# Four held weight-row pairs of the second feed-forward matrix: one transfer per two column halves instead of one per pair

## The chip, the cores and the metric

The kernel runs on one core of one Trainium2 chip. The metric is the device time of one execution, in microseconds (us). Before the change the median of three executions is 1231.31 us (1231.11 to 1232.1). The profile that is read below is one profiled execution, which took 1231.44 us. Engines go by short names: PE is the matrix engine and PEld its weight load, DVE the vector engine, ACT the scalar engine, POOL the GpSimd engine, SP the sync engine, whose queue issues most of the transfers.

## The reference

Two decoder layers over 256 tokens of width 1024. Each layer is a half-step feed-forward block, a mixer (gated attention and gated spatial mixing) and a second half-step feed-forward block, each followed by a layer norm:

```python
for l in range(DEPTH):                                   # DEPTH = 2
    h = _swiglu(x, ffn_w1[l, 0], ffn_w3[l, 0], ffn_w2[l, 0])
    x = _layernorm(ALPHA * x + 0.5 * h, ln_g[l, 0], ln_b[l, 0])
    h = _mixer(x, l, ...)
    x = _layernorm(ALPHA * x + h, ln_g[l, 1], ln_b[l, 1])
    h = _swiglu(x, ffn_w1[l, 1], ffn_w3[l, 1], ffn_w2[l, 1])
    x = _layernorm(ALPHA * x + 0.5 * h, ln_g[l, 2], ln_b[l, 2])

def _swiglu(x, w1, w3, w2):                              # w1, w3: 1024 x 2816, w2: 2816 x 1024
    return (jax.nn.silu(x @ w1) * (x @ w3)) @ w2
```

All is float32. The change touches `... @ w2`, which runs four times in the program, once in each feed-forward block.

## The kernel before

**Number format.** A float32 matrix product is made of three products of a shorter format. Each operand is split into a high part (a copy, on ACT) and a low part (operand minus high part, on DVE); PE then adds high x high, high x low and low x high (`three`, L214). A weight transfer is 1 MB, 128 x 2048 floats, into one of 4 `raw` buffers; `stream` splits it in two blocks of 1024 columns, each by one ACT copy (`whi`, L172) and one DVE subtraction (`wlo`, L174). High and low blocks live in two pools of 8 buffers each. A transfer can be issued when its `raw` buffer is free, that is after the last DVE subtraction that reads it.

**Order.** On PE the instructions run in the order in which the program writes them. On the other engines a planner puts each engine's instructions in an order ahead of time, by its own estimate of when operands are ready and, among those ready, by a priority that rises with each transfer (`step`), so that what the program writes earlier goes first. `issue_after` edges (`behind`, `after`) fix some places: in the stage after a norm, the second block of the second weight transfer and all of the third come behind the first token tile's normalisation (`norm.ends[0]`), those of the fourth behind the low part of the second transposed half (`norm.xlo[0, 1]`).

**The second feed-forward matrix.** Its 2816 rows are 22 tiles of 128 rows. Five pairs of row tiles (`SQ`) go through a seven-product scheme (`stream_s`, tiles `shi`, `slo`, `shh`, `shl`), whose sums stand in seven PSUM banks S1 to S7. The other six pairs (`PQ`) are plain. Output is two token tiles t by two column halves c of 512; the four results collect in `ends[t, c]`. The first two plain pairs are multiplied between the seven-product pairs. The other four are *held*: they are transferred and split, but multiplied only at the end, result by result: (0,0) with all four pairs, then (0,1), (1,0), (1,1). A pair and a column half take 6 matmuls, a result 24. Before the change a transfer holds one pair: its first column half in the first block, its second in the second block.

**Folds.** After the last seven-product pair, the banks S1, S5, S6 and S7 are folded into the residual on DVE: `ln.more` (L479, L477), `u` (L667) and `v` (L668), with one ACT copy (L664). In the program they stand ahead of the held transfers, but for the last three, which stand behind them.

**The norm and the next stage.** When a result is complete, `ln.part` adds it to the residual (L486) and takes its statistics (L491). After both halves of a token tile, `finish` aggregates (L498), takes an inverse square root in a chain of 128 x 1 operations (L186 to L192) and normalises the two halves (L502). PE then transposes the normalised halves (L546), ACT scales and copies them (L552, L179), DVE takes their low parts (L180), and the next stage's matmuls read them. The four transposes of a half stand at fixed places of the PE order: those of tile 0 after 6 and after 24 matmuls of the result (1,1), those of tile 1 in the next stage (after 30 and 42 of its matmuls). The next stage's first four weight transfers are split in blocks of 512 columns (`llo`, `lhi` for the first six, `wlo`, `whi` for the other ten). The last feed-forward block has no next stage; it writes the output.

Of the kernel before, what the change touches and what calls it, by code (L numbers as in the profile page):

```python
# [17 lines left out]
ALU = mybir.AluOpType  # L18
# [13 lines left out]
NS = 5  # L32
SQ = [(FB + 2 * p, FB + 2 * p + 1) for p in range(NS)]
PQ = [(k, k + 1) for k in (0, 2, *range(FB + 2 * NS, FT, 2))]
HEADS = 8
HD = 64
GROUPS = 8
# [19 lines left out]
def trunk(ctx, tc, x, xT, w13a, w13b, w2s, w2p, wb, wqk, wa, wbr, wo, gateb, sgug, sgub, sguwT, sgubias, lam, diffg,  # L57
# [18 lines left out]
    def name(s):  # L76
        serial[0] += 1
        return f"{s}_{serial[0]}"
# [32 lines left out]
    def step():  # L111
        chunk[0] += 1
        tc.cur_priority = chunk[0] * STEP
# [35 lines left out]
    def behind(ins):  # L149

        return tc.issue_after(ins) if ins is not None else nullcontext()

    def stream(src, width=CH, sub=HC, lent=(), after=(None, None)):

        step()
        raw = raw_pool.tile([P, CH], F32, tag="raw", name=name("raw"))
        nc.sync.dma_start(raw[:, :width], src)
        out = []  # L160
        for o in range(0, width, HC):
            if o // HC in lent:
                hi, lo = ([act.tile([P, 512], F32R, tag="slot", name=name(n)) for _ in range(2)] for n in ("lhi", "llo"))
                at = [(hi[j], lo[j]) for j in range(2)]
            else:
                hi = hi_pool.tile([P, HC], F32R, tag="hi", name=name("whi"))
                lo = lo_pool.tile([P, HC], F32R, tag="lo", name=name("wlo"))
                at = [(hi[:, p : p + sub], lo[:, p : p + sub]) for p in range(0, HC, sub)]
            for p, (h, w) in zip(range(0, HC, sub), at):
                r = raw[:, o + p : o + p + sub]  # L170
                with behind(latest[0]):
                    A.activation(h, r, AF.Copy)  # L172
                with behind(after[o // HC] or latest[1]):
                    V.tensor_tensor(out=w, in0=r, in1=h.bitcast(F32), op=ALU.subtract)  # L174
            out.append((hi, lo))
        return out
# [78 lines left out]
    def rows_p(ps, t, q, piece, xh, xl, c0=0, n=512, stop=False, start=False):  # L255

        for j, k in enumerate(q):
            wh, wl = (v[:, j * 512 + c0 : j * 512 + c0 + n] for v in piece)
            three(ps[:, :n], xh(k)[:, t * P : (t + 1) * P], xl(k)[:, t * P : (t + 1) * P], wh, wl,
                  start and j == 0, stop and j == 1)  # L260
        beat(n / 1024)
# [133 lines left out]
    b = side_bank()  # L395
# [169 lines left out]
    def ffn(l, f, i, norm, last=False):  # L565
        xh, xl = parts(both)
        h_hi, h_lo = ({q: act.tile([P, 512], F32R, tag="slot", name=name(n)) for q in PQ} for n in ("hhi", "hlo"))
        p_hi, p_lo = h_hi, h_lo
        h_hi, h_lo = ({k: d[q][:, j * T : (j + 1) * T] for q in PQ for j, k in enumerate(q)} for d in (h_hi, h_lo))
        hh, hl = h_hi.get, h_lo.get  # L570
# [59 lines left out]
        for j in range(FR, FT, 2):  # L630
            qa = s512("qa")
            for m, z in gemm_a2([w13a[l, f, j - FR + m] for m in range(2)], both, lambda m: t512("silu"), bank=side_bank):
# [5 lines left out]
        ln = Norm(l, i, 2.0 * ALPHA, 4.0 * EPS, qa[:, :1], last)  # L638
        S = {n: side_bank() for n in (3, 7, 4)}
        S.update({n: bank() for n in (1, 2, 5, 6)})  # L640
        ends = {(0, 0): [(S[2], 0, 512)], (0, 1): [(S[3], 0, 512)], (1, 0): [(S[4], 0, 512)],
                (1, 1): [(side_bank(), 0, 512)]}
        pair, held, plain = None, [], list(PQ)

        def plain_pair(hold):
            q = plain.pop(0)
            w = stream(w2p[l, f, PQ.index(q)])
            if hold:
                held.append((q, w))
                return  # L650
            for c in range(2):
                for t in range(NT):
                    for ps, o, m in ends[t, c]:
                        rows_p(ps, t, q, w[c], hh, hl, o, m, start=q == PQ[0] and t + c == 2)

        for n, q in enumerate(SQ):
            pair, w = stream_s(w2s[l, f, n], pair)
            for b in (1, 2, 5, 6, 3, 7, 4):
                three(S[b], *s_op[q][b], *w[b], n == 0, n == NS - 1 and b in (1, 5, 6, 7))
            beat(1.75)  # L660
            if n < 2:
                plain_pair(False)
        u, v = s512("u"), s512("v")
        A.activation(u, S[6], AF.Copy)  # L664
        ln.more(1, 0, S[7], ALU.subtract, ln.scale)
        ln.more(0, 0, S[1], ALU.add, ln.scale)
        V.tensor_tensor(out=u, in0=u, in1=S[1], op=ALU.add)  # L667
        V.tensor_tensor(out=v, in0=S[5], in1=u, op=ALU.subtract)  # L668
        ln.more(0, 1, v, ALU.add, ln.scale)
        while plain:  # L670
            plain_pair(True)
        ln.more(1, 1, v, ALU.add, ln.scale)
        ln.more(1, 0, u, ALU.add)
        ln.more(1, 1, S[7], ALU.add)
        for t in range(NT):
            for c in range(2):
                for ps, o, n in ends[t, c]:
                    for q, w in held:
                        rows_p(ps, t, q, w[c], hh, hl, o, n, stop=q == held[-1][0])
                    for o in ((0, 256) if last and (t, c) == (1, 1) else (0,)):  # L680
                        ln.part(t, c * 512 + o, ps[:, o : o + 256] if o or last and (t, c) == (1, 1) else ps, 1.0)
            ln.finish(t, ((2, 1.5), (2, 1))[t])
        return ln.close()

    def mixer(l, i, norm):
# [127 lines left out]

        for hp in range(HEADS // 2):
            qT = rope(wqk[l, hp, 0], HD ** -0.5)
            kT = rope(wqk[l, hp, 1], 1.0, hp == HEADS // 2 - 1)
            beside(attend(hp, qT, kT), 3.9)
# [100 lines left out]
def _layout(i):  # L918
    c = np.ascontiguousarray
    L = DEPTH  # L920
    f = {k: np.asarray(v) for k, v in i.items()}
    x = f["x"].reshape(T, D)
    o = {"x": x, "xT": c(x.reshape(T, KT, P).transpose(2, 1, 0)).reshape(P, KT * T)}

    def cols(w):

        k, n = w.shape[-2:]
        w = w.reshape(*w.shape[:-2], k // P, P, n // P, P)
        a = w.ndim
        return w.transpose(*range(a - 4), a - 2, a - 3, a - 4, a - 1)  # L930

    def pairs(w):

        w = cols(w)
        lead = w.shape[:-4]
        n = w.shape[-4]
        w = w.reshape(*lead, n // 2, 2, P, KT, P)
        a = w.ndim
        return c(w.transpose(*range(a - 4), a - 3, a - 4, a - 2, a - 1)).reshape(*lead, n // 2, P, CH)

    def halves(w):

        k, n = w.shape[-2:]
        w = w.reshape(*w.shape[:-2], k // P, P, n // 512, 512)
        a = w.ndim
        w = c(w.transpose(*range(a - 4), a - 2, a - 3, a - 4, a - 1))
        return w.reshape(*w.shape[:-2], (k // P) * 512)

    nb = FR * P
    w1, w3 = f["ffn_w1"], f["ffn_w3"]  # L950
    o["w13a"] = c(np.stack([cols(w1[..., nb:]), cols(w3[..., nb:])], axis=4)).reshape(L, 2, FT - FR, P, CH)
    o["w13b"] = c(np.stack([halves(w1[..., :nb]), halves(w3[..., :nb])], axis=2))
    w2 = f["ffn_w2"].reshape(L, 2, FT, P, 2, 512)

    def blocks(at):

        return c(np.stack([w2[:, :, k, :, h] for k, h in at], axis=3)).reshape(L, 2, P, CH)

    o["w2s"] = c(np.stack([blocks(((a, 0), (a, 1), (b, 1), (b, 0))) for a, b in SQ], axis=2))
    o["w2p"] = c(np.stack([blocks(((a, 0), (b, 0), (a, 1), (b, 1))) for a, b in PQ], axis=2))  # L960
    u, v, q, k, val, ga, gb = (f["w_in"][:, :, s * D : (s + 1) * D] for s in range(7))
    o["wb"] = np.stack([halves(w) for w in (v, val)], axis=1)
    o["wqk"] = np.stack([pairs(w) for w in (q, k)], axis=2)
    o["wa"] = np.stack([pairs(w) for w in (u, ga, gb)], axis=1)
    o["wbr"] = pairs(f["w_branch"])
    o["wo"] = halves(f["w_out"])
    o["gateb"] = c(f["gate_b"].reshape(L, 2, KT, P).transpose(3, 0, 1, 2))
    o["sgug"], o["sgub"] = f["sgu_ln_g"], f["sgu_ln_b"]
    o["sguwT"] = c(f["sgu_w"].transpose(0, 3, 1, 2)).reshape(L, P, GROUPS * P)
    o["sgubias"] = f["sgu_b"].reshape(L, GROUPS * P)  # L970
    o["lam"] = f["lam"]
    o["diffg"] = c(f["diff_ln_g"].T)
    o["lng"], o["lnb"] = f["ln_g"], f["ln_b"]
    for k in ("lng", "lnb"):
        o[k + "T"] = c(o[k].reshape(L, 3, KT, P).transpose(3, 0, 1, 2))
    inv = np.float32(ROPE_THETA) ** (-np.arange(0, HD, 2, dtype=np.float32) / np.float32(HD))
    ang = np.arange(T, dtype=np.float32)[:, None] * inv.astype(np.float32)[None, :]
    cs = np.cos(ang.astype(np.float64)).astype(np.float32).T
    sn = np.sin(ang.astype(np.float64)).astype(np.float32).T
    o["cosT"] = c(np.concatenate([cs, cs, cs, cs]))  # L980
    o["sinT"] = c(np.concatenate([-sn, sn, -sn, sn]))
    return o
# [18 lines left out]
```

## Time and profile before

| | before |
|---|---|
| median of three executions | 1231.31 us |
| profiled execution | 1231.44 us, of which 1229.7 us span |
| PE busy | 1212.5 us (99%), 6033 matmuls |
| DVE busy | 955.6 us (78%) |
| ACT busy | 814.1 us (66%) |
| DMA, mean over the span | 205 GB/s |
| granted PE clock | 0.999 |

The timelines have one row for an instruction, or for a run of equal ones: start in us from the span's start, duration in us, engine, line, operation, output <- inputs, shape, count; in brackets the engine's idle time ahead of it and what ended that. Matmuls overlap: one starts 0.23 us after the last and lasts 0.39 us. The waits view has one row for a pair of lines: waiting line <- line it waited for, total us, times, longest.

### The profile page before, as it was taken

Reading aid. Unit: us, or ns where it says so; the run is one execution under the profiler, and the core shown is the slowest. Engines: PE = TensorE matmul, PEld = TensorE weight load, DVE = VectorE, ACT = ScalarE, POOL = GpSimd, SP = SyncE. Lnnn points to the kernel's source line nnn. Section 1 sums busy time; section 2 is a strip of 40 time slices with the busy share of each in tenths; the row PEclk is TensorE's granted clock in tenths of the full one; section 3 lists DMA queues with packets and bytes.
Section 4 is the critical chain, followed back from the end, with each engine's and each line's share of the span. In section 5 each row is a group of like instructions: output and inputs, shape, how many; then the busy total and the mean of one; then the engine's idle time right before and its main releaser. Section 6 shows DMA issues by size and latency. Waiting matters only on the chain.

```text
span 1229.7 us, 16592 instructions
## 1 busy us (share of the span) xinstructions
PE 1212.5 (99%) x6033; PEld 1018.4 (83%) x6033; DVE 955.6 (78%) x1540; ACT 814.1 (66%) x1328; POOL 87.4 (7%) x184
## 2 busy tenths in 40 slices
PE   9999999999999999999999999999999999999997
PEld 8888878888888888888788888788888888888885
DVE  6668997886587985679975779978866879757796
ACT  7677666679665665776666776566786555667860
POOL 0100000234100000000000000002430000000000
PEclk9999999999999999999999999999999999999999
DMA  8976664654754657665757655755546456667450
GB/s 316 332 244 185 221 225 187 223 164 166 251 172 160 231 175 253 200 187 205 257 180 247 199 179 206 255 194 200 169 173 227 168 172 239 208 202 231 172 197 35
DMA packets 82339, 252.29 MB, mean 205 GB/s; under 512 B 47520, under 2 KB 48592, under 8 KB 55632
## 3 DMA queue, kind: packets, MB, share of 16 engines
q1 hardware_dynamic: 78288, 238.31, 57.6%
q0 software_dynamic: 3536, 12.13, 2.9%
q8 instruction: 47, 0.77, 0.3%
q10 hardware_dynamic: 432, 0.79, 0.2%
q14 instruction: 36, 0.29, 0.1%
HBM read 235.47 MB, written 1.05 MB: 192 GB/s over the span
## 4 chain that ended last, share of the span: by engine, by line
PE 85%; DVE 10%; issue 3%; ACT 2%; DVEq 0%; ACTq 0%
PE bank L214 31%; PE sbank L214 19%; PE bank L226 17%; PE bank L233 9%; DVE slo L298 3%; DVE wlo L174 2%; PE sbank L226 2%; PE bank L385 2%; PE sbank L734 1%; DVE raw L309 1%; ACT shi L296 1%; DVE raw L311 1%; PE sbank L546 1%; ACT columns L601 1%; DVE raw L310 1%
## 5 line engine op out<-in xcount | busy, mean ns | idle before, releaser
L174 DVE TENSOR_TENSOR wlo<-raw,whi 128x1024 fp32r<-128x1024 f32 (+1 forms) x402 | 441.4, 1115 | 156.5 <-ACT whi L172 116.8
L172 ACT ACTIVATE whi<-raw 128x1024 fp32r<-128x1024 f32 (+1 forms) x402 | 379.4, 966 | 185.5 <-PE bank L214 62.1
L214 PE MATMUL bank<-whi,x 128*128 128x512 f32 x840 | 264.5, 390 | 0.0
L214 PEld LDWEIGHTS bank<-whi,x 128*128 128x128 f32 x840 | 157.7, 188 | 32.5
L214 PE MATMUL bank<-wlo,x 128*128 128x512 f32 x420 | 163.5, 389 | 0.0
L214 PE MATMUL sbank<-whi,x 128*128 128x512 f32 x512 | 158.9, 389 | 0.0
L226 PE MATMUL bank<-x,whi 128*128 128x512 f32 x640 | 158.3, 395 | 0.0
L226 PEld LDWEIGHTS bank<-x,whi 128*128 128x128 f32 x640 | 116.5, 188 | 26.0 <-issue 2.7
L214 PEld LDWEIGHTS sbank<-whi,x 128*128 128x128 f32 x512 | 96.1, 188 | 19.9
L296 ACT ACTIVATE shi<-raw 128x1024 fp32r<-128x1024 f32 (+1 forms) x80 | 73.4, 947 | 52.0 <-DVE raw L311 26.4
L214 PE MATMUL sbank<-wlo,x 128*128 128x512 f32 x256 | 99.6, 389 | 0.0
L298 DVE TENSOR_TENSOR slo<-raw,shi 128x1024 fp32r<-128x1024 f32 (+1 forms) x80 | 85.3, 1088 | 14.1 <-ACT shi L296 13.3
L214 PEld LDWEIGHTS bank<-wlo,x 128*128 128x128 f32 x420 | 78.9, 188 | 16.0
L233 PE MATMUL bank<-x,wlo 128*128 128x256 f32 x640 | 85.8, 285 | 0.0
L233 PEld LDWEIGHTS bank<-x,wlo 128*128 128x128 f32 x640 | 81.5, 191 | 2.3
L234 ACT ACTIVATE r<-bank 128x256 f32<-128x256 f32 x112 | 41.8, 380 | 27.5 <-PE bank L233 27.5
L552 ACT ACTIVATE xf<-sbank,ln_b,ln_g 128x128 f32<-128x128 f32 x80 | 30.0, 456 | 40.8 <-PE sbank L546 40.8
L214 PE MATMUL sbank<-whi,hhi 128*128 128x512 f32 x144 | 56.4, 391 | 0.0
L214 PEld LDWEIGHTS sbank<-wlo,x 128*128 128x128 f32 x256 | 48.0, 188 | 10.0
L214 PE MATMUL sbank<-whi,hlo 128*128 128x512 f32 x144 | 56.1, 389 | 0.0
L214 PE MATMUL sbank<-wlo,hhi 128*128 128x512 f32 x144 | 56.1, 389 | 0.0
L445 POOL DMA_DIRECT2D bc<-in_lng x6 | 3.2, 529 | 711.8 <-DVE bc L444 711.8
(233 smaller groups left out, 1977.9 us busy)
## 6 DMA issues: line engine op xcount, KB each, us to landing
raw<-in_w13b SPq DMA_DIRECT2D x76, 1024.0 KB, 5.4
raw<-in_w2p SPq DMA_DIRECT2D x24, 1024.0 KB, 4.8
raw<-in_wa SPq DMA_DIRECT2D x24, 1024.0 KB, 5.3
raw<-in_w2s SPq DMA_DIRECT2D x20, 1024.0 KB, 4.9
raw<-in_wb SPq DMA_DIRECT2D x16, 1024.0 KB, 4.9
raw<-in_wqk SPq DMA_DIRECT2D x16, 1024.0 KB, 4.9
raw<-in_wbr SPq DMA_DIRECT2D x16, 1024.0 KB, 4.8
raw<-in_w13a SPq DMA_DIRECT2D x8, 1024.0 KB, 4.7
```

The lines of the kernel that those rows point to most:

```text
L172: A.activation(h, r, AF.Copy)
L174: V.tensor_tensor(out=w, in0=r, in1=h.bitcast(F32), op=ALU.subtract)
L214: PE.matmul(ps, xx, w, start=start and n == 0, stop=stop and n == 2)
L226: PE.matmul(b[-1], hi[:, k * P : (k + 1) * P], xc(k), start=k == 0, stop=False)
L233: PE.matmul(b[n][:, :T], lo[:, k * P : (k + 1) * P], xc(k)[:, :T], start=False, stop=k == KT - 1)
L234: emptied[0] = A.activation(r[:, s], b[n][:, T:], AF.Copy, scale=scale).ins
L296: A.activation(h, r, AF.Copy)
L298: V.tensor_tensor(out=w, in0=r, in1=h.bitcast(F32), op=ALU.subtract)
L309: V.tensor_tensor(out=raw[:, :1024], in0=raw[:, :1024], in1=raw[:, 512:1536], op=ALU.add)
L310: V.tensor_tensor(out=raw[:, 1024:1536], in0=raw[:, :512], in1=raw[:, 1024:1536], op=ALU.add)
L385: PE.matmul(ps[t][m], x[:, j, o + t * P : o + (t + 1) * P], y, start=k0 + j == 0 and o == 0 and y is hi, stop=k0 + j == KT - 1 and y is lo)
L552: A.activation(xf[:, s], b[:, s], AF.Identity, scale=self.gT[:, f], bias=self.bT[:, f])
```

## The change

`HELD = 4` names the number of held pairs. For these the layout in memory is changed: a transfer now holds the same column half of two pairs. Two transfers with the first halves of pairs 1, 2 and of 3, 4 stand ahead of the folds in the program, two with the second halves behind the first five folds. The first two folds swap places. The matmuls and their order stay; they take their blocks from `held[q, c]`. Number and size of transfers, splits and folds stay. The two plain pairs that are not held keep their layout.

```diff
+HELD = 4
...
-        pair, held, plain = None, [], list(PQ)
-
-        def plain_pair(hold):
-            q = plain.pop(0)
-            w = stream(w2p[l, f, PQ.index(q)])
-            if hold:
-                held.append((q, w))
-                return
+        pair, held = None, {}
+
+        def plain_pair(n):
+            q = PQ[n]
+            w = stream(w2p[l, f, n])
             for c in range(2):
...
-            if n < 2:
-                plain_pair(False)
+            if n < len(PQ) - HELD:
+                plain_pair(n)
         u, v = s512("u"), s512("v")
         A.activation(u, S[6], AF.Copy)
+        for m in range(HELD // 2):
+            q = PQ[len(PQ) - HELD + 2 * m :][:2]
+            held.update({(k, 0): w for k, w in zip(q, stream(w2p[l, f, len(PQ) - HELD + m]))})
+        ln.more(0, 0, S[1], ALU.add, ln.scale)
         ln.more(1, 0, S[7], ALU.subtract, ln.scale)
-        ln.more(0, 0, S[1], ALU.add, ln.scale)
         V.tensor_tensor(out=u, in0=u, in1=S[1], op=ALU.add)
         V.tensor_tensor(out=v, in0=S[5], in1=u, op=ALU.subtract)
         ln.more(0, 1, v, ALU.add, ln.scale)
-        while plain:
-            plain_pair(True)
+        for m in range(HELD // 2):
+            q = PQ[len(PQ) - HELD + 2 * m :][:2]
+            held.update({(k, 1): w for k, w in zip(q, stream(w2p[l, f, len(PQ) - HELD // 2 + m]))})
         ln.more(1, 1, v, ALU.add, ln.scale)
         ln.more(1, 0, u, ALU.add)
         ln.more(1, 1, S[7], ALU.add)
         for t in range(NT):
             for c in range(2):
                 for ps, o, n in ends[t, c]:
-                    for q, w in held:
-                        rows_p(ps, t, q, w[c], hh, hl, o, n, stop=q == held[-1][0])
+                    for q in PQ[-HELD:]:
+                        rows_p(ps, t, q, held[q, c], hh, hl, o, n, stop=q == PQ[-1])
...
-    o["w2p"] = c(np.stack([blocks(((a, 0), (b, 0), (a, 1), (b, 1))) for a, b in PQ], axis=2))
+    now, late = PQ[: len(PQ) - HELD], PQ[len(PQ) - HELD :]
+    o["w2p"] = c(np.stack([blocks(((a, 0), (b, 0), (a, 1), (b, 1))) for a, b in now]
+                          + [blocks([(k, h) for q in late[2 * m : 2 * m + 2] for k in q])
+                             for h in range(2) for m in range(HELD // 2)], axis=2))
```

## The prediction

> **What bounds the kernel now.** I read the page's busy times first, then who waited for whom, then the timelines of PE and DVE around the held pairs.
>
> ```profile
> span 1229.7 us, 16592 instructions
> PE 1212.5 (99%) x6033; PEld 1018.4 (83%) x6033; DVE 955.6 (78%) x1540; ACT 814.1 (66%) x1328; POOL 87.4 (7%) x184
> PE bank L214 <- DVE wlo L174: 10.9, 8, 1.5
> ```
>
> PE is the bound, and the matmuls do not change, so a gain can only be PE idle time. The last row (of PE's waits) says that nearly all of PE's waiting in mid-kernel is eight waits of a `bank` matmul for a low weight block: 10.9 us, two in each of the four feed-forward blocks. The first block's PE timeline shows the place (behind the dots: the same in the fourth block; the row ahead, of the chain that ended last, is a run of PE without waits).
>
> ```profile
> 92.93 21.76 PE bank L214 x96
> ...
> 160.32 0.39 PE L214 MATMUL bank<-whi,hhi 128*128 128x512 f32 x1
> 164.96 0.50 PE L214 MATMUL bank<-wlo,hhi 128*128 128x512 f32 x1 [1.53 <-DVE wlo L174]
> 167.83 0.50 PE L214 MATMUL bank<-wlo,hhi 128*128 128x512 f32 x1 [1.22 <-DVE wlo L174]
> 169.09 0.39 PE L214 MATMUL sbank<-whi,hhi 128*128 128x512 f32 x1
> ...
> 1196.15 0.39 PE L214 MATMUL bank<-whi,hhi 128*128 128x512 f32 x1
> 1204.89 0.39 PE L214 MATMUL sbank<-whi,hhi 128*128 128x512 f32 x1
> ```
>
> Result (0,0), 24 matmuls, runs from 160.32 to 169.09, 8.77 us. Unhindered matmuls start 21.76 / 96 = 0.227 us apart, 24 of them take 5.44, so 3.33 us are lost here, and 8.74 - 5.44 = 3.30 in the fourth block. That is more than the 2.75 in the brackets, because the idle is counted from the modelled end of a matmul. Four blocks: 13.3 us, the most that the change can bring. Now DVE at that place:
>
> ```profile
> 156.75 1.22 DVE L174 TENSOR_TENSOR wlo<-raw,whi 128x1024 fp32r<-128x1024 f32 x1
> 157.88 0.68 DVE L479 SCALAR_TENSOR_TENSOR xtok<-xtok,bank 128x512 f32<-128x512 f32 x1
> 158.48 2.35 DVE L174 TENSOR_TENSOR wlo<-raw,whi 128x1024 fp32r<-128x1024 f32 x2
> 160.75 0.68 DVE L479 SCALAR_TENSOR_TENSOR xtok<-xtok,sbank 128x512 f32<-128x512 f32 x1
> 161.35 0.68 DVE L667 TENSOR_TENSOR u<-u,bank 128x512 f32<-128x512 f32 x1
> 161.95 1.22 DVE L174 TENSOR_TENSOR wlo<-raw,whi 128x1024 fp32r<-128x1024 f32 x1
> 163.09 0.68 DVE L668 TENSOR_TENSOR v<-bank,u 128x512 f32<-128x512 f32 x1
> 163.69 1.22 DVE L174 TENSOR_TENSOR wlo<-raw,whi 128x1024 fp32r<-128x1024 f32 x1
> 164.82 0.68 DVE L479 SCALAR_TENSOR_TENSOR xtok<-xtok,v 128x512 f32<-128x512 f32 x1
> 165.42 3.49 DVE L174 TENSOR_TENSOR wlo<-raw,whi 128x1024 fp32r<-128x1024 f32 x3
> 168.83 0.68 DVE L479 SCALAR_TENSOR_TENSOR xtok<-xtok,v 128x512 f32<-128x512 f32 x1
> 169.43 0.68 DVE L477 TENSOR_TENSOR xtok<-xtok,u 128x512 f32<-128x512 f32 x1
> 170.03 0.68 DVE L477 TENSOR_TENSOR xtok<-xtok,sbank 128x512 f32<-128x512 f32 x1
> ```
>
> DVE has no gap: a split every 1.13 us, a fold every 0.60. Its eight splits alternate first half, second half, pair by pair, with five folds between. Result (0,0) wants only the first halves, which are the 1st, 3rd, 5th and 7th split: the third is done at 164.82 and the fourth at 167.7, and PE goes on at 164.96 and 167.83. So this stage is bound by DVE's order, not by its work.
>
> **The change part by part.**
>
> *First halves ahead.* The four first halves and then the folds have the higher priority. From 156.75 the four splits end at 157.9, 159.0, 160.2 and 161.3. PE, unhindered, reads their low blocks from 160.55, 161.9, 163.3 and 164.6. Even with all five folds ahead of the last (5 x 0.60), it ends at 164.3, so the stall goes under either order. Their transfers:
>
> ```profile
> 156.86 0.33 SPq L159 DMA_DIRECT2D raw<-in_w2p  x1
> 155.48 3.89 ACT L172 ACTIVATE whi<-raw 128x1024 fp32r<-128x1024 f32 x4
> 163.03 2.01 ACT L172 ACTIVATE whi<-raw 128x1024 fp32r<-128x1024 f32 x2 [1.28 <-DMA raw<-in_w2p]
> ```
>
> ACT's four copies from 155.48 are pairs 1 and 2; the fourth held transfer, issued at 156.86, is the one that ACT waits for until 163.03 (about 6.1 us). The second held transfer has landed before 157.4, when ACT's third copy reads it. After the change it holds the first halves of pairs 3 and 4, so all four first halves are there in time. Sizes, number and issuing queue stay, so this costs nothing. On SP, the next stage's first two transfers wait for the first two held buffers, free at 159.0 and 161.3 instead of 159.6 and 163.1: a little earlier. POOL is not touched. Swapping the two folds costs nothing, both being ready by then.
>
> *Second halves behind.* Folds 161.3 to 164.3, then the second halves end at 165.4, 166.6, 167.7 and 168.8. PE starts (0,1) at 160.32 + 5.44 = 165.76 and reads their low blocks at 166.0, 167.4, 168.7, 170.1: slack 0.6, 0.8, 1.0, 1.3 us. The last two come with the transfer that lands at 163.0 and cost ACT 2.0, to 165.0, in time. I take no stall; the bound above is dealt with as a rival.
>
> So PE is 3.3 us ahead after (0,0). The cover for that is DVE. The total of splits and folds is the same, and DVE leaves them at 168.83 as before. In the last block nothing follows that DVE lacks time for (it sits idle 2.65 us ahead of the second result's sum), and I take the full 3.3:
>
> ```profile
> 1210.56 0.69 DVE L486 TENSOR_TENSOR xtok<-xtok,sbank 128x512 f32<-128x512 f32 x1 [2.65 <-PE sbank L214]
> ```
>
> *The next late thing in the other three blocks* is the norm of tile 0:
>
> ```profile
> L174 DVE TENSOR_TENSOR llo<-raw,lhi 128x512 fp32r<-128x512 f32 x6 | 3.8, 679 | 0.0
> 172.43 2.48 DVE L174 TENSOR_TENSOR llo<-raw,lhi 128x512 fp32r<-128x512 f32 x4
> 178.49 0.27 DVE L191 TENSOR_SCALAR nwa<-nwy,ve 128x1 f32<-128x1 f32 x1
> 178.80 0.21 DVE L192 TENSOR_SCALAR nwy<-nwa,nwy 128x1 f32<-128x1 f32 x1
> 179.05 1.00 DVE L502 TENSOR_SCALAR xtok<-xtok,mv,nwy 128x512 f32<-128x512 f32 x2
> 181.34 0.60 PE L546 MATMUL sbank<-ident,xtok 128*128 128x128 f32 x4
> ...
> 186.11 0.69 DVE L486 TENSOR_TENSOR xtok<-xtok,sbank 128x512 f32<-128x512 f32 x1 [0.66 <-PE sbank L214]
> 188.75 0.27 DVE L191 TENSOR_SCALAR nwa<-nwy,ve 128x1 f32<-128x1 f32 x1
> 188.94 0.68 DVE L180 TENSOR_TENSOR x<-xf,x 128x512 fp32r<-128x512 f32 x1
> 189.53 0.21 DVE L192 TENSOR_SCALAR nwy<-nwa,nwy 128x1 f32<-128x1 f32 x1
> 191.77 0.99 DVE L502 TENSOR_SCALAR xtok<-xtok,mv,nwy 128x512 f32<-128x512 f32 x2
> 193.20 0.60 PE L546 MATMUL sbank<-ident,xtok 128*128 128x128 f32 x4
> ```
>
> PE transposes the first half of tile 0 at 181.34, from then on at 181.34 - 3.33 = 178.01. But L502 ends that half at about 179.6 (start 179.05, half of the pair), and up to there DVE works without a pause on a set of work that the change leaves alone: splits, folds, two sums, the norm's chain and six `llo` splits. If nothing shrinks, PE waits until 179.65 and 1.69 of the 3.33 stay. Something shrinks: four `llo` splits stood together only because the second result was not there yet; now it comes 3.3 us earlier, the chain has priority, and they fall between its steps. What that is worth stands in tile 1's chain: with a 0.68 us operation between them two steps start 0.78 apart (188.75, 189.53), without one 0.31 (178.49, 178.80). An operation there costs 0.47, against 0.60 in a row, so four save 0.5: 2.2 us stay. None moved is the lower bound, 1.69; all left until after the norm the upper one, 3.33.
>
> By the Trainium skill ("VectorE: DVE Perf Modes", section "The DRAIN you can't avoid") the next vector operation does not start until the pipeline has emptied, whatever stands between. Taken so, moving the `llo` splits saves nothing, the three blocks keep 1.69 each and the time would be 1223.1 us. The trace disagrees: rows 0.68 long start 0.60 apart, and the interleaved one costs 0.47.
>
> *Tile 1's norm.* Its sum was ready at 186.11 and is now at 183.9. DVE's work from tile 0's norm to there was 5.35 us (180.05, where L502 ends, to 185.45, 0.66 ahead of the sum) and has 4.3 us now (from 179.55), so about two splits fall into tile 1's chain, at 0.47 each: L502 starts at 191.77 - 2.2 + 0.95 = 190.5 and its first half is done at 191.0, just when PE comes for it (193.20 - 2.2 = 191.0). A third would take 0.5 us. So 1.7 to 2.2 stay; I take 2.0. Later work is shifted as a whole: behind it no wait of PE is in the list above.
>
> *Sum.* 3.3 + 3 x 2.0 = 9.3 us. Profiled execution 1231.44 (span 1229.7 and 1.74 around it, taken as unchanged, 0.13 above the median) - 9.3 = 1222.1 us.
>
> **The rivals.**
>
> *All of it stays.* If the planner leaves `llo` splits until tile 0 is normalised (they are read only in the next stage), three blocks keep 3.0 to 3.3: 12.3 to 13.3 us, 1218.1 to 1219.1. For it: the priorities favour the norm. Against: in tile 1's chain the planner put a split in every gap it could.
>
> *Most is lost again at tile 1 and in the next stage.* The third and fourth weight transfer's eight splits (4.8 us) may be ordered so that tile 1's chain or the next stage's matmuls stand still. If each block keeps 0.5 and the last 3.3, 4.8 us: 1226.6. For it: DVE shows only 0.66 us of idle there. Against: it idles 2.68 us behind them, at 193 to 196 (its row: [2.68 <-ACT x L179]), so work that is put off finds room.
>
> ```profile
> 196.04 0.69 DVE L180 TENSOR_TENSOR x<-xf,x 128x512 fp32r<-128x512 f32 x1 [2.68 <-ACT x L179]
> ```
>
> *Nothing is saved between the chain's steps.* An operation that falls between two steps then costs its full 0.60 and tile 0's norm ends where it did: 1.69 in three blocks, 3.3 in the last, 8.4 us, 1223.1. For it: rows of like length stand 0.60 apart everywhere in the run of splits and folds. Against: 0.47 in tile 1's chain. It is the lower part of the case of the sum, with a fifth of its chance. (The rule of the skill named above says the same.)
>
> *Slower: the second halves come too late.* If the planner expects their transfers late, it fills DVE with what else is ready: three folds, the first sum and its statistics, six `llo` splits, 11 x 0.60 = 6.6 us. The last second half would end at 175.4 against a need at 170.1: a stall of 5.3 for the 3.3 won, 2 us lost in each of three blocks; in the last, without the six `llo` splits, the stall is 1.7 and 1.6 of the 3.3 stay. In sum 3 x 2.0 - 1.6 = 4.4 us slower, 1235.8. It decides from eight such operations ahead (1.3 + 3.3 = 4.6 us). Against: all have lower priority, and before the change the last three splits run without one between them although their transfer lands last.
>
> *The change does nothing* (the planner keeps today's order of splits): 1231.4. Against: a split needs its transfer, and the first two now bring first halves.
>
> **How the numbers follow.** The case of the sum, 6.5 to 11.2 us gained (1220.2 to 1224.9): 0.56 (0.11 of it nothing saved between the steps). All of it stays (1218.0 to 1220.2): 0.17. Most lost again (1224.9 to 1228.8): 0.14. Nothing, within 0.2% (2.5 us, about what a measurement of this kernel can tell from no change): 0.07. Slower by more: 0.06. Range 1218.2 to 1226.6, which leaves out about 0.2. Faster 0.87, same 0.07, slower 0.06.
>
> **What would show it.** Right: PE has no wait for `wlo` between the first held matmul and (0,1), and (0,0) takes 5.4 us; DVE shows four `wlo` splits together ahead of the folds; a new PE wait of 1.1 to 1.6 us at L546, for L502, in three blocks, none in the last; `llo` splits between the steps of tile 0's chain. Wrong: a wait for `wlo` at the `sbank` matmuls of (0,1); a wait at the next stage's first matmuls; L546 with no wait (then all of it stayed).

## The result and the profile after

| | before | after |
|---|---|---|
| median of five executions | 1231.31 us (1231.01 to 1232.1) | 1226.29 us (1224.17 to 1227.77) |
| profiled execution, span | 1231.44, 1229.7 | 1224.48, 1222.7 |
| granted PE clock of the executions | 0.999 (profiled) | 1.000, 0.999, 1.000, 0.999, 0.997 |

The ratio is 0.9955 (95% interval 0.994 to 0.9969): 5.0 us faster by the medians, 7.0 us in the profiled execution, where 9.3 were forecast. The executions now lie 3.6 us apart, and the longer ones have the lower clock.

The page's head after the change, then the new rows of PE's waits in mid-kernel (line numbers are one higher, so L503 is the normalisation and L547 the transposes):

```profile
span 1222.7 us, 16592 instructions
PE 1209.9 (99%) x6033; PEld 1018.2 (83%) x6033; DVE 954.5 (78%) x1540; ACT 813.1 (66%) x1328; POOL 88.0 (7%) x184
```

```profile
PE sbank L547 <- DVE xtok L503: 4.1, 2, 2.2
PE sbank L547 <- issue: 2.0, 1, 2.0
```

The eight waits for `wlo` are gone from the list. Three waits at the transposes have come, 6.1 us (one is put down to "issue", but stands at the same instruction). PE's timeline in the first block, then the transposes of tile 0 in the second and third block and the held pairs of the fourth:

```profile
160.08 0.39 PE L215 MATMUL bank<-whi,hhi 128*128 128x512 f32 x1
...
165.52 0.39 PE L215 MATMUL sbank<-whi,hhi 128*128 128x512 f32 x1
...
179.88 0.63 PE L547 MATMUL sbank<-ident,xtok 128*128 128x128 f32 x4 [1.95 <-issue]
...
191.74 0.60 PE L547 MATMUL sbank<-ident,xtok 128*128 128x128 f32 x4
...
605.85 0.66 PE L547 MATMUL sbank<-ident,xtok 128*128 128x128 f32 x4 [2.17 <-DVE xtok L503]
...
786.27 0.66 PE L547 MATMUL sbank<-ident,xtok 128*128 128x128 f32 x4 [1.91 <-DVE xtok L503]
...
1192.48 0.39 PE L215 MATMUL bank<-whi,hhi 128*128 128x512 f32 x1
...
1197.92 0.39 PE L215 MATMUL sbank<-whi,hhi 128*128 128x512 f32 x1
```

Result (0,0) takes 5.44 us instead of 8.77: the stall has gone in full. PE arrives at the transposes of tile 0 at about 177.9 and waits until 179.88; before the change it came at 181.34. So PE is 1.46 us ahead there, of which 0.24 stem from before 160 (160.32 to 160.08): the block keeps 1.2 of its 3.3 us. The 0.24 are not put down to the change: over the twelve traces of this case the held pairs of the first block start anywhere from 160.01 to 160.60, and both ends of that are kernels with the new layout. At tile 1 (191.74 against 193.20) PE is still 1.46 ahead. DVE in the same block:

```profile
156.52 4.62 DVE L175 TENSOR_TENSOR wlo<-raw,whi 128x1024 fp32r<-128x1024 f32 x4
...
162.85 1.22 DVE L175 TENSOR_TENSOR wlo<-raw,whi 128x1024 fp32r<-128x1024 f32 x1
...
164.59 1.22 DVE L175 TENSOR_TENSOR wlo<-raw,whi 128x1024 fp32r<-128x1024 f32 x1
...
166.32 2.35 DVE L175 TENSOR_TENSOR wlo<-raw,whi 128x1024 fp32r<-128x1024 f32 x2
...
177.02 0.21 DVE L193 TENSOR_SCALAR nwy<-nwa,nwy 128x1 f32<-128x1 f32 x1
177.15 0.68 DVE L487 TENSOR_TENSOR xtok<-xtok,sbank 128x512 f32<-128x512 f32 x1
177.74 0.27 DVE L192 TENSOR_SCALAR nwa<-nwy,ve 128x1 f32<-128x1 f32 x1
177.92 0.68 DVE L492 BATCH_NORM_STATS2 st<-xtok 128x6 f32<-128x512 f32 x1
178.52 0.20 DVE L193 TENSOR_SCALAR nwy<-nwa,nwy 128x1 f32<-128x1 f32 x1
178.64 0.68 DVE L175 TENSOR_TENSOR llo<-raw,lhi 128x512 fp32r<-128x512 f32 x1
179.24 1.00 DVE L503 TENSOR_SCALAR xtok<-xtok,mv,nwy 128x512 f32<-128x512 f32 x2
```

The four first halves stand together ahead of the folds, the second halves between them. The normalisation of tile 0 starts at 179.24, against 179.05 before, although DVE reached the held pairs 0.23 us earlier. Between the steps of its chain stand now not only `llo` splits but the sum of result (1,0) (L487) and its statistics (L492), which stood behind the normalisation before.

### The profile page after: what moved, and what is told of

Its sections match the earlier page's. It is cut to its first block, busy times and chain, and to the rows that moved or that the text cites. A ratio compares the mean times of both kernels' runs of the same rounds, so it can differ in the third digit from the quotient of the medians.

```text
span 1222.7 us, 16592 instructions
## 1 busy us (share of the span) xinstructions
PE 1209.9 (99%) x6033; PEld 1018.2 (83%) x6033; DVE 954.5 (78%) x1540; ACT 813.1 (66%) x1328; POOL 88.0 (7%) x184
## 3 DMA queue, kind: packets, MB, share of 16 engines
HBM read 235.47 MB, written 1.05 MB: 193 GB/s over the span
## 4 chain that ended last, share of the span: by engine, by line
PE 89%; DVE 7%; issue 2%; ACT 1%; DMA 0%; DVEq 0%; ACTq 0%
PE bank L215 34%; PE sbank L215 21%; PE bank L227 17%; PE bank L234 9%; PE sbank L227 2%; PE bank L386 2%; DVE wlo L175 2%; DVE slo L299 1%; PE sbank L736 1%; PE sbank L547 1%; PE sbank L234 1%; DVE llo L175 1%; PE sbank L785 1%; PE sbank L866 1%; DVE raw L310 1%
```

## The experiments

Theory A: in the three blocks with a next stage, DVE's work ahead of the normalisations caps the gain. Theory C: the spread of the executions comes from PE's clock, which falls after a wait of about 2 us in some of them. Each kernel was timed in five rounds beside the kernel before.

**The change taken apart.** In the first kernel the two transfers of first halves stand behind the five folds, with the new layout:

```diff
-        for m in range(HELD // 2):
-            q = PQ[len(PQ) - HELD + 2 * m :][:2]
-            held.update({(k, 0): w for k, w in zip(q, stream(w2p[l, f, len(PQ) - HELD + m]))})
         ln.more(0, 0, S[1], ALU.add, ln.scale)
...
         ln.more(0, 1, v, ALU.add, ln.scale)
+        for m in range(HELD // 2):
+            q = PQ[len(PQ) - HELD + 2 * m :][:2]
+            held.update({(k, 0): w for k, w in zip(q, stream(w2p[l, f, len(PQ) - HELD + m]))})
```

> The changed kernel's layout (one column half of two pairs in a transfer), but the two transfers of first halves stand behind the first five folds in the program, right ahead of the second halves. Theory A: the first halves are still the first four splits; with some folds between them the last ends near 163 us, ahead of its need at 164.4, and the work ahead of tile 0's normalisation is the same: the time of the changed kernel, 1224.5, within 0.5 us. Rival E (the place ahead of the folds is what counts): a wait of a bank matmul for a low block comes back and the time lies between, 1226 to 1231.

1226.04 us (1224.38 to 1227.56), the times of the changed kernel, with no wait for `wlo` although three folds now stand ahead of the fourth first half. The place ahead of the folds is not what counts. The second keeps the old layout and moves the held transfers ahead of the folds:

```diff
         A.activation(u, S[6], AF.Copy)
+        while plain:
+            plain_pair(True)
...
         ln.more(0, 1, v, ALU.add, ln.scale)
-        while plain:
-            plain_pair(True)
```

> The kernel before, with its layout (one pair in a transfer), but the four held transfers moved ahead of the folds in the program. The fourth first half is the seventh split of eight: 156.75 + 7 x 1.13 = 164.7 without folds between them, or 165.1 by its transfer (landed at 163.0, ACT copy 0.97, split 1.13), against a need at 164.6. Theory A: a wait of about 0.5 us remains at result (0,0), and the wait at tile 0's transposes is shorter by as much, so three blocks gain as in the changed kernel and only the last loses 0.5: about 1225.0. Rival F (the column-half layout is what brings the gain): the stall at (0,0) stays for the most part, 1229 to 1231.

1225.11 us (1224.53 to 1225.55). PE's timeline of the first block:

```profile
165.65 0.50 PE L214 MATMUL bank<-wlo,hhi 128*128 128x512 f32 x1 [0.70 <-DVE wlo L174]
180.78 0.63 PE L546 MATMUL sbank<-ident,xtok 128*128 128x128 f32 x4 [1.45 <-issue]
```

In the first three blocks result (0,0) takes 6.43, 5.78 and 5.77 us, 1.66 more in sum than in the changed kernel; the waits at the transposes are 1.45, 1.40 and 1.40 us, 1.78 less in sum than 1.95, 2.17 and 1.91. So over the three blocks, if not in each, what PE waits more at the held pairs it waits less at the transposes. The last block has nothing to hide it: (0,0) takes 6.10 us there, and 0.66 is lost. By the times, either half of the change alone brings about as much as both, as long as something else caps the gain.

**Work put off behind tile 0's normalisation.** First the six `llo` splits, in the stage behind a feed-forward block (`norm.defer`):

```diff
             after[1:3] = (None, norm.ends[0]), (norm.ends[0], norm.ends[0])
+            if norm.defer:
+                after[:2] = [(norm.ends[0], norm.ends[0])] * 2
```

> The changed kernel, with all six llo splits of the next stage ordered behind tile 0's normalisation. Theory A (in three of four blocks the gain is capped by the DVE work that stands ahead of tile 0's normalisation): DVE reaches it at about 175.7 instead of 179.2 us, PE's waits of 1.9 to 2.2 us at the transposes go; the put-off splits lengthen tile 1's chain by about three operations of 0.47 us, which gives a wait of about 0.6 at tile 1's transposes. Each block then keeps about 2.7 of 3.3 us: 1220.0 us. Rival B (the wait only moves: what is put off is missed in the next stage at once): no change against the changed kernel, 1224.5, with waits of about 2 us at tile 1's transposes or at the next stage's first matmuls. Theory C on the spread of the changed kernel's runs (1224.2 to 1227.8 us with a granted clock of 1.000 to 0.997): a single wait of 2 us makes the clock fall in some executions; without it all runs have 1.000 and lie within 1 us.

1225.9 us (1224.75 to 1227.47), as the changed kernel: rival B was right. PE's waits, and the timeline of PE's transposes and of DVE in the first block:

```profile
PE sbank L549 <- DVE xtok L505: 6.0, 3, 2.0
```

```profile
177.69 0.60 PE L549 MATMUL sbank<-ident,xtok 128*128 128x128 f32 x4
191.71 0.66 PE L549 MATMUL sbank<-ident,xtok 128*128 128x128 f32 x4 [2.02 <-DVE xtok L505]
...
175.37 1.01 DVE L505 TENSOR_SCALAR xtok<-xtok,mv,nwy 128x512 f32<-128x512 f32 x2
183.50 0.68 DVE L489 TENSOR_TENSOR xtok<-xtok,sbank 128x512 f32<-128x512 f32 x1
191.11 1.00 DVE L505 TENSOR_SCALAR xtok<-xtok,mv,nwy 128x512 f32<-128x512 f32 x2
```

Tile 0 is normalised 3.9 us earlier and PE does not wait for it. But the work that was put off all stands ahead of tile 1's normalisation: the sum of the last result comes at 183.50, 1.2 us after PE went on to the next transposes (182.26), and the chain behind it takes 7.6 us (183.50 to 191.11) instead of 5.66. PE waits 2.02 us there. Then the sum of result (1,0) and its statistics alone:

```diff
-            with behind(self.xlo.get((0, 0))):
+            with behind(self.xlo.get((0, 0)) or (self.ends[0] if t else None)):
```

> The changed kernel, with the sum of result (1,0) and its statistics ordered behind tile 0's normalisation (two of the operations that stand ahead of it). Theory A: two operations at about 0.5 us each leave DVE's work ahead of the normalisation, PE's wait there falls from 2.0 to about 1.0 us, each of three blocks keeps 2.3 instead of 1.2 to 1.4 us: 1221.3. Rival B (what is put off is missed later): 1224.5. Rival D (the wait is not set by DVE's work but by the end of the second result on PE and the length of the norm's chain): no change, 1224.5.

1224.31 us (1223.65 to 1224.36). The transposes of the two tiles:

```profile
179.40 0.63 PE L547 MATMUL sbank<-ident,xtok 128*128 128x128 f32 x4 [1.00 <-issue]
...
191.97 0.66 PE L547 MATMUL sbank<-ident,xtok 128*128 128x128 f32 x4 [0.56 <-DVE xtok L503]
```

The first wait fell from 1.95 to 1.0 us as forecast (to 1.24 and 0.96 in the next two blocks), which shows that DVE's work ahead of it sets it; half of that came back at tile 1 (0.56, 0.55 and 0.56), which I had not counted. The edge holds for the mixer's norms too, where no wait came of it. So the work has to leave both chains. The idle time that DVE has there is behind tile 1's normalisation.

**The fourth transfer's splits behind tile 1's normalisation.** One kernel has this edge alone (`after[3]` below), another with two more: the second transfer's two `llo` splits (`after[1]`) and the sum of (1,0), both behind tile 0's normalisation.

```diff
+            if norm.defer:
+                after[1] = norm.ends[0], norm.ends[0]
...
-                    after[3] = [norm.xlo.get((0, 1))] * 2
+                    after[3] = [norm.ends[1] if norm.defer else norm.xlo.get((0, 1))] * 2
...
-            with behind(self.xlo.get((0, 0))):
+            with behind(self.xlo.get((0, 0)) or (self.ends[0] if t else None)):
```

> The changed kernel with only the last of the three edges: the fourth transfer's splits behind tile 1's normalisation. Theory A: tile 1's normalisation comes about 1.4 us earlier, but in the changed kernel PE does not wait there; the wait of 2 us at tile 0 stays, so no change: 1224.2 to 1227.8 us, by the number of clock drops. Rival G (tile 1's chain is what holds the changed kernel): 1.4 us less in each of three blocks, 1220.3.

1225.83 us (1223.88 to 1225.96): as the changed kernel, so tile 1's chain alone does not hold it.

> The changed kernel with three ordering edges more: the sum of result (1,0) and the two llo splits of the second transfer behind tile 0's normalisation, the fourth transfer's four splits behind tile 1's normalisation instead of only behind the low part of tile 0's second half. Theory A (DVE's work ahead of each of the two normalisations sets when PE may go on, and DVE has room only behind the second): tile 0's normalisation starts near 177.4 and tile 1's near 189.0, PE waits 0.2 to 0.3 us at the first and not at the second, each of three blocks keeps 3.0 of 3.3 us: 1219.1 us, all executions with a clock of 0.999 or 1.000 and within 0.7 us. Rival B (the wait is conserved whatever is put off, as the llo run suggests): 1223 to 1225, with waits at tile 1's transposes or in the next stage's matmuls on the fourth transfer.

1218.86 us (1218.63 to 1219.23), ratio to before 0.9898 (0.9885 to 0.9912), clock 1.000 in every execution. Its only row of PE's waits at the transposes, and DVE's timeline in the first block:

```profile
PE sbank L549 <- DVE xtok L505: 0.3, 1, 0.3
```

```profile
177.44 1.00 DVE L505 TENSOR_SCALAR xtok<-xtok,mv,nwy 128x512 f32<-128x512 f32 x2
189.05 1.00 DVE L505 TENSOR_SCALAR xtok<-xtok,mv,nwy 128x512 f32<-128x512 f32 x2
189.97 2.49 DVE L175 TENSOR_TENSOR wlo<-raw,whi 128x512 fp32r<-128x512 f32 x4
192.79 0.69 DVE L181 TENSOR_TENSOR x<-xf,x 128x512 fp32r<-128x512 f32 x1 [0.34 <-ACT x L180]
```

The four splits fill what was idle at 193 to 196 before, and 12.4 of the 13.3 us are there. How much the edge on the two `llo` splits gives by itself was not measured. The three edges on the kernel before:

> The three edges on the kernel before, without the change. Theory A: before the change PE is late by itself (it waits for the first halves at result (0,0)) and waits for neither normalisation, so the edges bring nothing: 1231.2 us, within 0.6. Rival: the edges bring the gain of the last runs by themselves, 1226 or less.

```profile
PE bank L214 <- DVE wlo L174: 10.8, 8, 1.5
```

1231.25 us (1230.84 to 1232.07), ratio 1.0 (0.9991 to 1.0009): alone the edges bring nothing. Last, the edges with the old layout and the held transfers ahead of the folds, beside the three-edge kernel on the same chip:

> The old layout with the four held transfers ahead of the folds, and the three ordering edges of the spread kernel. In the run without the edges result (0,0) took 6.43, 5.78, 5.77 and 5.42 us in the four blocks against 5.44 unhindered, because the last first half stands in the transfer that lands last. Theory A: with the edges no wait at the transposes hides that any more, so the column-half layout is now worth about 0.7 us in the first block and 0.1 to 0.4 in the next two: about 1220.1 us against 1218.9. Rival H (the layout is worth nothing, the order of folds and splits is all): 1218.9, within 0.3.

> The kernel with the change and the three edges once more, beside the one with the old layout: 1218.9 us, within 0.5, with a clock of 1.000.

1219.83 us (1219.21 to 1220.35) against 1218.88 (1218.49 to 1219.15). Result (0,0) of the first block, in the old layout:

```profile
160.24 0.39 PE L214 MATMUL bank<-whi,hhi 128*128 128x512 f32 x1
...
166.02 0.39 PE L214 MATMUL sbank<-whi,hhi 128*128 128x512 f32 x1
```

5.78 us against 5.44, and 5.75 to 5.76 in the other three blocks: the layout by column halves is worth about 1 us of the 12.3. The rest comes from the order, that of the splits against the folds and the three edges together; the first of the two alone gave 6 us, the second nothing.

**The clock.** The profiled execution of the kernel with the first halves behind the folds took 1226.18 us and has one drop of the clock, while the profiled execution of the changed kernel has none. PE's timeline, and the busy times of three stretches (the column behind POOL's is PE's granted clock):

```profile
178.05 0.39 PE L215 MATMUL sbank<-whi,hlo 128*128 128x512 f32 x1
180.38 1.04 PE L547 MATMUL sbank<-ident,xtok 128*128 128x128 f32 x4 [1.94 <-issue]
...
182.08 0.63 PE L215 MATMUL sbank<-whi,hlo 128*128 128x512 f32 x1
182.50 0.63 PE L215 MATMUL sbank<-whi,hhi 128*128 128x512 f32 x1
...
183.78 0.44 PE L215 MATMUL sbank<-whi,hhi 128*128 128x512 f32 x1
184.06 0.39 PE L215 MATMUL sbank<-wlo,hhi 128*128 128x512 f32 x1
```

```profile
180.00:182.00 2.00, 1.62 (x6) 1.54 (x7) 2.00 (x5) 0.54 (x2) 0.00 (x0) 0.61 0.16 66
182.00:184.00 2.00, 2.00 (x6) 1.53 (x5) 1.48 (x3) 1.60 (x4) 0.00 (x0) 0.54 0.39 86
184.00:186.00 2.00, 2.00 (x10) 1.64 (x10) 1.56 (x3) 0.00 (x0) 0.00 (x0) 1.00 0.98 414
```

Behind the wait of 1.94 us matmuls start 0.43 us apart instead of 0.23, for 3.4 us (180.38 to 183.78). That costs 1.6 us: the transposes of the next half come 6.18 us later (186.56, the same view) instead of 4.57 (179.88 to 184.45 in the changed kernel). The kernel with the `llo` splits behind has another, behind its wait of 2.04 us in the second block, which ends at 617.73:

```profile
617.00:619.00 2.00, 1.27 (x6) 1.16 (x7) 1.10 (x3) 0.54 (x2) 0.00 (x0) 0.81 0.98 381
619.00:621.00 2.00, 2.00 (x6) 1.53 (x5) 0.34 (x1) 1.60 (x4) 0.00 (x0) 0.50 0.66 274
621.00:623.00 2.00, 2.00 (x11) 1.58 (x10) 0.35 (x1) 0.00 (x0) 0.00 (x0) 0.84 0.03 12
```

If the clock is taken as either full or half, these means give an estimate of the stretch at half: 0.76 + 2.00 + 0.64 = 3.4 us, from 618.24, 0.5 us after PE went on. The two means of the other trace, 0.61 and 0.54, give 1.56 + 1.84 = 3.4 us too, but from 180.44, within 0.1 us of the end of the wait. So the stretch has the same length in both, and does not begin at a fixed time after the wait. A kernel with longer waits, by two more operations in tile 0's chain:

```diff
+                if t == 0 and self.defer:
+                    for _ in range(2):
+                        z = s512("late")
+                        V.tensor_scalar(out=z, in0=y[:, :512], scalar1=0.0, scalar2=var, op0=ALU.mult, op1=ALU.add)
+                        var = z[:, :1]
```

> The changed kernel with two dependent 128x512 DVE operations more in tile 0's norm chain (they copy the variance), which lengthen PE's wait at tile 0's transposes by about 1.2 us, from 2.0 to 3.2, in three blocks. By the waits alone 3.6 us more than the changed kernel's best executions: 1228.1. Theory C (PE's granted clock falls to half for about 3.4 us behind a wait that is long enough, which costs 1.6 us each time; at 2 us it happens in some waits): a longer wait is followed by it nearly always, three times 1.6 us more, 1231 to 1233 us with a clock of 0.996. Rival (the clock drops have nothing to do with the wait): 1228.1 to 1231 with the clock as in the changed kernel.

```profile
180.87 0.63 PE L553 MATMUL sbank<-ident,xtok 128*128 128x128 f32 x4 [2.97 <-issue]
...
607.54 0.66 PE L553 MATMUL sbank<-ident,xtok 128*128 128x128 f32 x4 [2.92 <-DVE xtok L509]
...
789.00 0.66 PE L553 MATMUL sbank<-ident,xtok 128*128 128x128 f32 x4 [2.93 <-DVE xtok L509]
```

1228.71 us (1227.09 to 1232.04, eleven executions). The times fall in four groups: three at 1227.1 to 1227.3 (clock 0.999 to 1.000), three at 1228.6 to 1228.7, two at 1230.5 and 1231.0, three at 1231.5 to 1232.0 (0.996). Read as none to three drops, that is 16 drops in 33 waits (three in each execution). "Nearly always" was wrong: about half by this reading, and the profiled execution had none. Counted the same way, in steps of 1.6 us above the lowest, the four kernels with waits of 2 us (the changed one, first halves behind the folds, `llo` behind, fourth transfer behind) have about 16 in 60. The executions of each kernel whose waits there are 1.45 us and less stay within 1.2 us. Shown are two drops in the traces, each behind a wait of 2 us, out of twelve such waits; the three waits of 2.9 us in a trace brought none. That each group of times is a number of drops, and that longer waits bring more of them, is inferred from times and mean clocks. Against the rival that the drops have nothing to do with the waits stands that the clock is 0.998 or lower in seven of these eleven executions, and 1.000 in all eight of the three-edge kernel, which has no such wait.

## Why the prediction was right or wrong

The median, 1226.29 us, lies 0.3 us inside the range, in the stretch that the prediction gave to "most is lost again" (0.14); the profiled execution, 1224.48, lies in the case of the sum. So the mechanism held where the stall was and failed in what followed, and that the median stayed in the range is in part luck.

*First halves ahead, second halves behind:* right. (0,0) takes 5.44 us in all four blocks of the trace, no wait for `wlo` is left, and the second halves' slack held. The robustness claim (any order of folds and first halves will do) is borne out by one more order, that of the kernel with the first halves behind the folds.

*The last block keeps 3.3:* right. (0,0) takes 5.44 us there (1192.48 to 1197.92) instead of 8.74, and nothing behind it takes the 3.3 back: 1204.89 became 1197.92 at the start of (0,1), 7.0 us, and the end of the span is 7.0 earlier too.

*The other three keep 2.0:* wrong, 1.2, 1.05 and 1.3. Before the change the transposes of the second and third block stood here:

```profile
608.36 0.60 PE L546 MATMUL sbank<-ident,xtok 128*128 128x128 f32 x4
...
790.05 0.60 PE L546 MATMUL sbank<-ident,xtok 128*128 128x128 f32 x4
```

They came 2.51 us (to 605.85) and 3.78 us (to 786.27) earlier. The new waits are 1.91 to 2.17 us, where 1.1 to 1.6 were named as the sign of being right. The step that failed is "up to there DVE works without a pause on a set of work that the change leaves alone". I moved `llo` splits between the chain's steps, but not what else becomes ready when PE runs 3.3 us ahead: result (1,0) is complete before tile 0 is normalised, and the planner puts its sum and statistics into the same chain. The forecast had it start 0.5 us before 179.05, at 178.55; it started at 179.24, which is 179.48 in the times of before (0.24 later). The miss of 0.93 is two operations at 0.47 us, and the kernel that sends just these two behind the normalisation has a wait shorter by 0.95 (1.95 to 1.00). With 2.5 us less in three blocks and the 0.24 from the start the profiled execution gives 7.0 instead of 9.3.

*0.47 us for an operation between two steps:* right. Two steps with the sum between them start 0.72 us apart (177.02, 177.74), against 0.25 without (178.80, 179.05 before). So the rival that nothing is saved between the steps is out. The prediction set the sentence of the Trainium skill ("VectorE: DVE Perf Modes", section "The DRAIN you can't avoid") against the trace, but left out what the same paragraph adds, that an operation that is not held starts earlier. With that the starts 0.60 us apart of rows 0.68 long are no disagreement with the page as a whole.

*Tile 1's norm:* no wait in the changed kernel, as forecast. The normalisation started at 190.30, or 190.54 in the times of before, where 190.5 was forecast; PE, held longer at tile 0, came at 191.98 in those times (191.74 + 0.24), 1.0 us after the 191.0 of the forecast, so there was room to spare that the forecast did not have. With less waiting at tile 0 it does hold PE, as two runs showed. The rival "most is lost again" had the mechanism, and "it idles behind them, so work that is put off finds room" holds only if an edge sends it there: the planner fills the chain first.

*The time around it:* missing. The forecast had no term for the clock. From the profiled execution to the median it is another 1.8 us (1224.48 to 1226.29), which by the mean clocks (1.000 and 0.999) fits about one drop; the execution of the median has no trace. The Trainium skill ("TensorE: Matmul & The Clock Gate", section "Part 1: The HAM clock gate (the "warmup" mystery)") has PE's clock at half after at least one idle window of about 3.4 us, the windows running freely. The 3.4 us at half rate in both traces agree with that length; that a wait of 1.94 us is enough does not agree with its threshold. Before, two waits of 1.53 and 1.22 us stood with some matmuls between them, and the times of that kernel show nothing of the kind.

## What to carry to other kernels

A wait taken away on the bounding engine is worth only what the next wait leaves: run the feeding engine's queue forward, and include in it the work that becomes ready sooner because the bound runs ahead, for an order made by readiness will put it into the chain that is now late. Operations sent behind one chain turn up in the next one; the ones to move are those that can go to a stretch where the engine is idle, and then by an explicit edge. Several short waits and one long wait need not be the same on the matrix engine: here waits of 2 us were followed by half a clock in two traces and, by the times of the executions, in about a quarter of the cases.

## What the runs showed of the hardware

PE's granted clock can fall to half for 3.4 us behind a wait of 1.94 or 2.04 us, at a cost of 1.6 us: two traces show it. Read from the times of the executions alone, it came behind about a quarter of the waits of 2 us and half of those of 2.9 us, and behind none of 1.45 us and less. By the same reading it differs from execution to execution of one kernel, and the five executions of the changed kernel lie 3.6 us apart where those of before lie 1.1. What decides it in a single wait stays open.
